# One core, two layers: routing and gates of an expert layer, with weights split two blocks ahead, TensorE in program order, 20 row dots in routing and gate copies in 16-byte runs

## Chip, cores and metric

One core of a Trainium2 chip runs the whole kernel. Its engines work side by side and wait for each other through semaphores: TensorE (PE, matrix products; PEld is its weight load), VectorE (DVE), ScalarE (ACT), GpSimd (POOL) and SyncE (SP, which here only issues DMAs). ACT and POOL issue DMAs too, from the same queue of instructions in which their other work stands. The metric is the device time of one execution in microseconds; less is better.

## The reference, cut

512 tokens of width 1024 pass two layers. Each layer is a mixer (a recurrence in the first, attention in the second) and then a feed-forward part with 16384 experts, of which each token uses 128. Only this part is touched:

```python
q = (xc @ q_w).reshape(TOKEN_CHUNK, PEER_HEADS, 2, PEER_HALF)
s1 = jnp.einsum('thd,hnd->thn', q[:, :, 0], subkey1)
s2 = jnp.einsum('thd,hnd->thn', q[:, :, 1], subkey2)
v1, i1 = lax.top_k(s1, PEER_TOPK)
v2, i2 = lax.top_k(s2, PEER_TOPK)
cand = (v1[..., :, None] + v2[..., None, :]).reshape(TOKEN_CHUNK, PEER_HEADS, PEER_TOPK * PEER_TOPK)
top_s, top_c = lax.top_k(cand, PEER_TOPK)
e1 = jnp.take_along_axis(i1, top_c // PEER_TOPK, axis=-1)
e2 = jnp.take_along_axis(i2, top_c % PEER_TOPK, axis=-1)
expert = e1 * PEER_KEYS + e2
g = jax.nn.softmax(top_s, axis=-1)
u = jnp.take(expert_u, expert, axis=0)
act = jax.nn.gelu(jnp.einsum('thkd,td->thk', u, xc), approximate=False)
return jnp.einsum('thk,thkd->td', g * act, jnp.take(expert_v, expert, axis=0))
```

## The kernel before

**Two ways to compute the experts.** Tokens are taken in four tiles of 128. The last tile is computed by gathering: for each of its 128 experts per token a row of `expert_u` is fetched by an indirect DMA and multiplied with the token on DVE, and the same for `expert_v`. The other three tiles (`nd` = 3, 384 tokens) are computed densely: all 16384 experts, 128 at a time, as matrix products, and what a token did not choose is multiplied with a gate of zero. Of these 384 tokens, 32 (`XT`) are a mixed case: their first product is done by gathering, in `looked_up`, as 32 dots (L1037) of 1024 numbers on 128 partitions. So the dense first product has 352 columns.

**float32 by halves.** Every float32 operand of PE is split into a rounded high part and a low rest; a product is three matmuls. Splitting a block of weights takes one ACT instruction (`whi`, L185) and one DVE subtraction (`wlo`, L187). `Stream` does this in the order of use: `take` hands out a block and first splits on to `ahead` blocks beyond it; there are four buffers of each half. The raw weights come in pairs of blocks, 1 MB, through SP.

**The part that is changed**, L1208 to L1221, runs once in each layer, between the search for the best keys (`queries`) and the loop over all experts (L1284). It goes over the 54 blocks of `FIRST[NEARLY:]`. For each it calls `first_up` (L831): `proj_t` makes the 24 matmuls of 128x352 (L513 to L515), ACT applies the gelu into `at` (L835, two buffers), and an ACT-issued DMA stores it to `ascr` (L836) for the loop that follows. After each block, `bg.pump(GP)` lets generators run whose work is mostly DVE's: each `yield` gives a cost, and the pump goes on until the costs used reach the credit, 5.35 per block. What is left at the end runs in `bg.finish()`. The generators, in order:

- `route(t)` for the four tiles (the tile with the 32 mixed tokens first): it turns positions among the candidates into the indices `e1`, `e2` by comparing with the constants `thr`, `row`, `col` and adding up (`route_half`), and makes the softmax `gt`.
- `looked_up`, dealt out between the steps of the others by `between_steps`: `natural` (L255, 16 transposing matmuls into one PSUM bank, L257 copies out) makes the tokens row-wise, then 32 dots. Their rows are fetched by POOL, 13 of them into buffers that the gates will use later, two per dot; the rest into three buffers `xr` once routing is over. At the end the results are copied together (L1042), scaled, and the largest is spread by one matmul (L1054) and copied to `most_all`, which the loop reads.
- `dense_gates(t)` for three tiles, eight passes each over 16 tokens, 24 passes in all. DVE compares with a ramp to get two sets of zeros and ones, `p2` (L1123) and `p1` (L1126), and multiplies `p1` with the two halves of the gate into `pg` (L1134, twice). `products` then multiplies `p2` and `pg` on PE, 32 matmuls of 128x128 (L1108) into four PSUM banks; ACT evicts each bank into `st` (L1110), 512 numbers per partition, written 64 bytes apart; `st` goes to `gscr` in DRAM by one ACT-issued DMA of 1 MB (L1112), and one eighth of it is kept by L1111. A pass's products are put after the next pass's `p2` and `p1` in the program.

The order in which one engine's instructions stand is decided by a scheduler when the kernel is built, by its own estimate of times; what is wrapped in `keep_in_program_order` (or `pin`) keeps its place in the program. PE's instructions in this part are not pinned before. The loop over experts (L1284) has its own background, the gathered tile, dealt out by `PUMPS`: a credit for a block whose first product must still be computed, and one for a block that was stored.

Of the kernel before, what the change touches and what calls it, by code (L numbers as in the profile page):

```python
# [17 lines left out]
S = 512  # L18
# [20 lines left out]
NEARLY = sum(EARLY)  # L39
PUMPS = ((4.55, 1.5), (4.2, 1.35))  # L40
AHEAD = 6
GP = 5.35
GSCALE = 32768.0
# [205 lines left out]

def natural(g, psum, h, tokens, out, half):  # L250

    ps = psum.tile([128, 4, 128], F32, name="nat", tag="tp", bufs=1)
    for k in range(4):
        for i, part in enumerate(h):
            g.nc.tensor.matmul(ps[:, k, :], tokens(part[:, half * 4 + k]), g.identr,  # L255
                               start=(i == 0), stop=(i == 1))
    g.nc.scalar.activation(out[:, half * 512:(half + 1) * 512].rearrange("p (a b) -> p a b", b=128), ps, AF.Copy)  # L257
# [247 lines left out]

def proj_t(g, psum, h, n=S, bank=None):

    nc = g.nc
    whi, wlo = g.stream.take()
    hhi, hlo = h  # L510
    ps = (psum.tile([128, S], F32, name="pacc", tag="acc") if bank is None else bank)[:, :n]
    for k in range(KD):
        nc.tensor.matmul(ps, whi[:, k, :], hhi[:, k, :n], start=(k == 0), stop=False)  # L513
        nc.tensor.matmul(ps, whi[:, k, :], hlo[:, k, :n], start=False, stop=False)  # L514
        nc.tensor.matmul(ps, wlo[:, k, :], hhi[:, k, :n], start=False, stop=(k == KD - 1))  # L515
    return ps
# [289 lines left out]
def peer(g, norm_fn, u, v, grow_fn, gate_rows, between, last_rows, nd, cost):  # L806
# [10 lines left out]
    with pool(tc, name="pk", bufs=1) as pk:  # L817
# [13 lines left out]
        def first_up(psum, c, ps=None):  # L831

            ps = proj_t(g, psum, h, NX) if ps is None else ps
            at = pa.tile([128, NX], F32, name="at", tag="at")
            A.activation(at, ps, AF.Gelu)  # L835
            nc.scalar.dma_start(ascr[FIRST.index(c)], at)  # L836
# [28 lines left out]
        HK = PH * QK  # L865
        thr = rs.tile([128, TOPK, HK], BF, name="thr")
        row = rs.tile([128, TOPK, HK], BF, name="rowlen")
        col = rs.tile([128, TOPK, HK], BF, name="col")

# [68 lines left out]
        def route_half(t, q):  # L938
# [15 lines left out]
            n = QK * (q + 1)  # L954
            shp = [128, n, HK]
            tab = [x[:, :n] for x in env["tab"]]
# [4 lines left out]
            ge, ge2 = (rs.tile([128, TOPK, HK], BF, name=x, tag=x)[:, :n] for x in ("ge", "ge2"))  # L961
            V.tensor_tensor(ge, posb.unsqueeze(1).to_broadcast(shp), thr[:, :n], op=OP.is_ge)
            V.tensor_tensor(ge2, ge, row[:, :n], op=OP.mult)
            V.tensor_tensor(ge, ge, tab[0], op=OP.mult)
            fold(ge, n, ranks(e[0], q))
            yield (6.0, 7.2)[q]
            j = rs.tile([128, HK], BF, name="j", tag="j")
            fold(ge2, n, j.rearrange("p (h k) -> p h k", h=PH))
            V.tensor_sub(j, posb, j)
            V.tensor_tensor(ge, j.unsqueeze(1).to_broadcast(shp), col[:, :n], op=OP.is_equal)  # L970
            V.tensor_tensor(ge, ge, tab[1], op=OP.mult)
            fold(ge, n, ranks(e[1], q))
            yield (5.5, 8.4)[q]

        def route(t):
# [16 lines left out]
            yield 2.2  # L992

        def looked_up(t, pu, pw, psum):
# [15 lines left out]
            def fetch(j):  # L1010
                if j < 13:
                    k = (0, 0, 1, 1, 2, 2, 3, 4, 4, 4, 4, 4, 4)[j]
                    if k == 4:
                        if j % 2:
                            env["pair"] = pw.tile([128, 2, D], F32, name="two", tag="st", bufs=3)
                        r = env["pair"][:, (j + 1) % 2]
                    else:
                        r = (pu if k == 3 else pw).tile([128, D], F32, name="rowx", tag=("p2", "pg0", "pg1", "p1")[k])
                else:
# [12 lines left out]
            for j in range(XT):  # L1032
                for _ in range(2):
                    if len(rows) < (XT if "xr" in env else 13):
                        fetch(len(rows))
                r = rows[j]
                pin(V.scalar_tensor_tensor(r, r, 1.0, hn, op0=OP.mult, op1=OP.mult, accum_out=act[:, j:j + 1]))  # L1037
                yield 1.35 if "xr" in env else 2.9
            A.activation(act, act, AF.Gelu)
# [11 lines left out]
            V.tensor_scalar(gt[own], back[own], inv[own], None, op0=OP.mult)  # L1051
            V.tensor_copy(back, most.to_broadcast([128, 128]))
            ps = psum.tile([128, 4, 128], F32, name="tp", tag="tp", bufs=1)
            T.matmul(ps[:, 0, :XT], back, g.ident[:, 128 - XT:], start=True, stop=True)  # L1054
            A.activation(most_all, ps[:, 0, :XT], AF.Copy)

        def between_steps(main, side, credit):
# [15 lines left out]
        def dense_gates(t, pu, pw, psum, todo):  # L1073
# [19 lines left out]
            pin(V.scalar_tensor_tensor(gp[1], tp[:, 2, :], GSCALE, gp[0], op0=OP.mult, op1=OP.subtract))  # L1093
            gdup = []
            for i in range(2):
                d = pu.tile(shp, F16, name=f"gdup{i}", tag=f"gdup{i}")
                A.activation(d, gp[i].unsqueeze(2).to_broadcast(shp), AF.Copy)
                gdup.append(d)
            yield 1.5

            def products(n, p2, pg):
                st = pw.tile([128, 128, 16], F32, name="st", tag="st", bufs=3)
                for q in range(4):
                    gps = psum.tile([128, 4, 128], F32, name="gps", tag="sps", bufs=4)
                    for r in range(4):
                        tk_ = q * 4 + r
                        for i in range(2):
                            T.matmul(gps[:, r, :], p2[:, tk_, :, :].rearrange("p a b -> p (a b)"), pg[i][:, :, tk_, :],  # L1108
                                     start=(i == 0), stop=(i == 1))
                    A.activation(st[:, :, q * 4:q * 4 + 4].rearrange("p e t -> p t e"), gps, AF.Copy, scale=1.0 / GSCALE)  # L1110
                A.activation(gts[0][:, n], st[:, 0:8, :], AF.Copy)  # L1111
# [5 lines left out]
            for b in range(8):  # L1117
# [10 lines left out]
                if todo:  # L1128
                    products(*todo.pop())
                    yield 0.1  # L1130
                pg = []
                for i in range(2):
                    x = pw.tile(shp, F16, name=f"pg{i}", tag=f"pg{i}")
                    pin(V.tensor_tensor(x, p1, spread(gdup[i]), op=OP.mult))  # L1134
                    pg.append(x)
                    yield 1.15
                todo.append((t * 8 + b, p2, pg))
# [64 lines left out]
        with pool(tc, name="ups", bufs=1, space=PSUM) as psum:  # L1202
# [540 lines left out]
```

## Time and profile before

| | us |
|---|---|
| median of 3 runs (3107.61 to 3116.07) | 3108.65 |
| the profiled execution | 3111.14 |
| its span | 3109.4 |
| around the span | 1.7 |
| granted clock, mean | 0.984 |

The span is divided, by what runs, into the recurrence, layer 0's queries, its routing and gates (437 to 744 us), its loop over experts (to 1516), attention, and the same three parts of layer 1 (routing and gates 2031 to 2338, the loop to the end). In the rows below a group is a line, an engine and an operation, with output and input names, shapes, count, busy us in total, mean ns of one, and then the idle time of that engine just before them and what ended it. ACTq marks a DMA issue in ACT's queue, with the time that the issue took. Instructions of one engine overlap a little, so a duration is somewhat longer than the distance to the next start.

### The profile page before, as it was taken

How to read it: one execution, taken by the hardware profiler on the slowest of the kernel's cores; microseconds unless marked ns; L12 is line 12 of the kernel's file. 1: busy time of each engine (PE TensorE's matmuls, PEld its weight loads, DVE VectorE, ACT ScalarE, POOL GpSimd, SP SyncE). 2: the span in 40 equal slices, each digit the busy share in tenths (PEclk: the TensorE clock that was granted, in tenths of full speed). 3: DMA queues.
4: the chain of work that ended last, by engine and by line, in shares of the span. 5: the costliest groups of instructions: out<-in, count | busy, mean ns of one | idle time of the engine just before them, and what ended most of it. 6: DMA issues, size and time to landing. Idle time of an engine off the chain costs nothing.

```text
span 3109.4 us, 45245 instructions
## 1 busy us (share of the span) xinstructions
PE 2987.0 (96%) x16232; PEld 2631.3 (85%) x16232; DVE 2618.9 (84%) x5368; ACT 1486.9 (48%) x2432; POOL 1053.1 (34%) x906
## 2 busy tenths in 40 slices
PE   8999999989999999999999999999889999999999
PEld 6778899878888888888777778999779888888887
DVE  8867987887988989999679878889886889888897
ACT  6664254677333333333458843255674333333332
POOL 1001422211655525664011003421204555445552
PEclk9999999989999999999999999999999999999999
DMA  7454347878999999998332133367979999999996
GB/s 294 176 186 168 111 150 295 271 250 286 418 383 383 393 358 387 386 383 338 136 113 83 63 149 128 116 254 254 286 241 363 363 385 378 374 347 383 361 361 247
DMA packets 307938, 855.28 MB, mean 275 GB/s; under 512 B 27296, under 2 KB 162496, under 8 KB 268928
## 3 DMA queue, kind: packets, MB, share of 16 engines
q1 hardware_dynamic: 67280, 388.77, 33.0%
q0 software_dynamic: 98624, 354.99, 30.2%
q10 hardware_dynamic: 141808, 108.63, 10.6%
q8 instruction: 127, 2.08, 0.3%
q14 instruction: 99, 0.81, 0.1%
HBM read 767.93 MB, written 83.51 MB: 274 GB/s over the span
## 4 chain that ended last, share of the span: by engine, by line
PE 50%; DVE 23%; DMA 9%; issue 8%; ACT 8%; ACTq 2%; POOL 0%; DVEq 0%; SPq 0%; POOLq 0%
PE vacc L1271 16%; PE pacc L515 9%; PE pacc L513 9%; PE pacc L514 8%; DMA at<-ascr 7%; DVE wlo L187 4%; DVE accg L1179 4%; DVE rows L1162 3%; ACT st L1110 2%; DVE mw L220 1%; ACTq L836 1%; ACT whi L185 1%; PE gps L1108 1%; DVE at L1257 1%; DVE wl L1264 1%
## 5 line engine op out<-in xcount | busy, mean ns | idle before, releaser
L515 PE MATMUL pacc<-hhi,wlo 128*128 128x352 f32 (+1 forms) x2600 | 892.6, 344 | 20.5 <-DVE wlo L187 20.3
L513 PE MATMUL pacc<-hhi,whi 128*128 128x352 f32 (+1 forms) x2600 | 898.0, 345 | 9.0 <-ACT at L835 5.8
L185 ACT ACTIVATE whi<-wraw 128x1024 fp32r<-128x1024 f32 (+1 forms) x646 | 661.7, 1033 | 494.1 <-PE pacc L514 272.9
L514 PE MATMUL pacc<-hlo,whi 128*128 128x352 f32 (+1 forms) x2600 | 892.4, 343 | 0.0
L187 DVE TENSOR_TENSOR wlo<-wraw,whi 128x1024 fp32r<-128x1024 f32 (+2 forms) x580 | 698.2, 1210 | 162.0 <-ACT whi L185 153.8
L1271 PE MATMUL vacc<-whi,wh 128*128 128x512 f32 x1536 | 598.3, 390 | 0.0
L1271 PE MATMUL vacc<-whi,wl 128*128 128x512 f32 x1536 | 597.7, 389 | 0.0
L1271 PE MATMUL vacc<-wlo,wh 128*128 128x512 f32 x1536 | 597.7, 389 | 0.0
L515 PEld LDWEIGHTS pacc<-hhi,wlo 128*128 128x128 f32 x2600 | 495.7, 191 | 50.6 <-DVE wlo L187 27.6
L513 PEld LDWEIGHTS pacc<-hhi,whi 128*128 128x128 f32 x2600 | 496.4, 191 | 40.2 <-ACT at L835 6.3
L514 PEld LDWEIGHTS pacc<-hlo,whi 128*128 128x128 f32 x2600 | 497.2, 191 | 26.0
L1261 ACT ACTIVATE wh<-at 128x384 fp32r<-128x384 f32 x256 | 134.2, 526 | 786.2 <-DVE at L1257 639.2
L1149 POOL DMA_INDIRECT rows<-in_l_v_dram,ei x256 | 370.9, 1449 | 306.5 <-DVE accg L1179 259.7
L1149 POOL DMA_INDIRECT rows<-in_l_u_dram,ei x256 | 371.4, 1451 | 269.5 <-DVE rows L1162 217.0
L1271 PEld LDWEIGHTS vacc<-whi,wl 128*128 128x128 f32 x1536 | 288.3, 188 | 60.2
L1271 PEld LDWEIGHTS vacc<-wlo,wh 128*128 128x128 f32 x1536 | 288.7, 188 | 55.8
L1271 PEld LDWEIGHTS vacc<-whi,wh 128*128 128x128 f32 x1536 | 288.4, 188 | 55.9
L1179 DVE SCALAR_TENSOR_TENSOR accg<-rows,act,accg 128x1024 f32<-128x1024 f32 x254 | 324.4, 1277 | 0.1
L1162 DVE SCALAR_TENSOR_TENSOR rows<-rows,hn 128x1024 f32<-128x1024 f32 x256 | 304.8, 1217 | 2.7 <-DMA rows<-in_l_u_dram,ei 2.6
L1257 DVE TENSOR_TENSOR at<-at,gtile 128x384 f32<-128x384 f32 x256 | 140.8, 552 | 151.8 <-DMA at<-ascr 144.9
L1110 ACT ACTIVATE st<-gps 128x512 f32<-128x512 f32 x192 | 185.0, 1105 | 70.8 <-PE gps L1108 50.7
L1021 POOL DMA_INDIRECT rowx<-in_l_u_dram,eix x52 | 75.5, 1452 | 354.7 <-DVE rowx L1037 187.5
(335 smaller groups left out, 3691.6 us busy)
## 6 DMA issues: line engine op xcount, KB each, us to landing
wraw<-in_l_uT_dram SPq DMA_DIRECT2D x128, 1024.0 KB
wraw<-in_l_vp_dram SPq DMA_DIRECT2D x128, 1024.0 KB
gscr<-st ACTq DMA_DIRECT2D x48, 1024.0 KB
gtile<-gscr SPq DMA_DIRECT2D x90, 512.0 KB
mw<-in_l_ffn_mw_dram POOLq DMA_DIRECT2D x48, 512.0 KB
ascr<-at ACTq DMA_DIRECT2D x136, 176.0 KB
at<-ascr ACTq DMA_DIRECT2D x136, 176.0 KB
mw<-in_l_mix_mw_dram POOLq DMA_DIRECT2D x32, 512.0 KB
```

What stands on the lines that cost most here:

```text
L185: self.pin(nc.scalar.activation(hi, raw, AF.Copy))
L187: self.pin((nc.gpsimd if self.on_pool else nc.vector).tensor_sub(lo, raw, hi))
L513: nc.tensor.matmul(ps, whi[:, k, :], hhi[:, k, :n], start=(k == 0), stop=False)
L514: nc.tensor.matmul(ps, whi[:, k, :], hlo[:, k, :n], start=False, stop=False)
L515: nc.tensor.matmul(ps, wlo[:, k, :], hhi[:, k, :n], start=False, stop=(k == KD - 1))
L1110: A.activation(st[:, :, q * 4:q * 4 + 4].rearrange("p e t -> p t e"), gps, AF.Copy, scale=1.0 / GSCALE)
L1149: i = nc.gpsimd.indirect_dma_start(out=rows, out_offset=None, in_=src, in_offset=bass.IndirectOffsetOnAxis(ap=ei[:, j:j + 1], axis=0))
L1162: V.scalar_tensor_tensor(r, r, 1.0, hn, op0=OP.mult, op1=OP.mult, accum_out=act[:, j:j + 1]))
L1179: i = V.scalar_tensor_tensor(acc, r, w, acc, op0=OP.mult, op1=OP.add)
L1257: pin(V.tensor_tensor(at.rearrange("p (b t) -> p b t", t=16), at.rearrange("p (b t) -> p b t", t=16), gts[c // 8][:, :, c % 8, :], op=OP.m ...
L1261: pin(A.activation(wh, at, AF.Copy))
L1271: T.matmul(acc[t][d], x[:, ts], y[:, d, :], start=(i == 0 and x is wh and y is vh), stop=(i == PK - 1 and x is wl))
```

## The change

- `proj_t` gets a `pin`; in this part the first matmul of each block keeps its place in the program, and so does the first gate matmul of each of the four banks in `products`.
- `g.stream.ahead` is 2 during this part, 3 again after it. `at` has four buffers.
- The credit `GP` is 4.81 by its formula; routing's costs and its dots are scaled by `RS` = 1.6. 20 of the 32 dots (`RX`) are to run in routing, from the same 13 buffers in rotation; a row is fetched after each dot, three ahead.
- `natural` in `looked_up` uses the four banks of the products. The matmul and copy for `most_all` become a generator of their own, `most_of`, behind all others.
- The two `pg` products are one of twice the size; the two `gdup` tiles are one.
- The evictions write four neighbouring numbers (16 bytes) at a time, and read PSUM in the order that this asks for.
- The constants `thr`, `row`, `col` are kept once and not once per head; DVE reads them with a repeated dimension.
- `PUMPS` of layer 0's loop: 4.55 and 1.5 become 4.35 and 1.42.

```diff
-PUMPS = ((4.55, 1.5), (4.2, 1.35))
+PUMPS = ((4.35, 1.42), (4.2, 1.35))
-GP = 5.35
+RX = 20
+RS = 1.6
+GP = ((54.4 + 1.3 * RX) * RS + 119.7 + 1.35 * (XT - RX)) / (NFIRST - 13)
...
-            at = pa.tile([128, NX], F32, name="at", tag="at")
+            at = pa.tile([128, NX], F32, name="at", tag="at", bufs=4)
...
-        thr = rs.tile([128, TOPK, HK], BF, name="thr")
+        thr = rs.tile([128, TOPK, QK], BF, name="thr")
...
-            V.tensor_tensor(ge, posb.unsqueeze(1).to_broadcast(shp), thr[:, :n], op=OP.is_ge)
-            V.tensor_tensor(ge2, ge, row[:, :n], op=OP.mult)
+            V.tensor_tensor(heads(ge), ranked(posb), fixed(thr), op=OP.is_ge)
+            V.tensor_tensor(heads(ge2), heads(ge), fixed(row), op=OP.mult)
...
-            yield (6.0, 7.2)[q]
+            yield RS * (2.75, 3.4)[q]
...
-                natural(g, psum, h, lambda x: x[:, ND - 128:ND], hn, half)
+                natural(g, psum, h, lambda x: x[:, ND - 128:ND], hn, half, "sps", 4)
...
-                for _ in range(2):
-                    if len(rows) < (XT if "xr" in env else 13):
-                        fetch(len(rows))
+                while len(rows) <= j:
+                    if "xr" in env:
+                        for n in range(RX, RX + 3):
+                            fetch(n)
+                    yield 0.1
                 r = rows[j]
                 pin(V.scalar_tensor_tensor(r, r, 1.0, hn, op0=OP.mult, op1=OP.mult, accum_out=act[:, j:j + 1]))
-                yield 1.35 if "xr" in env else 2.9
+                n = len(rows)
+                if n < (min(RX, j + 14) if n < RX or "xr" not in env else min(XT, max(RX, j + 1) + 3)):
+                    fetch(n)
+                yield 1.35 if "xr" in env else RS * 1.3
...
-                            T.matmul(gps[:, r, :], p2[:, tk_, :, :].rearrange("p a b -> p (a b)"), pg[i][:, :, tk_, :],
-                                     start=(i == 0), stop=(i == 1))
-                    A.activation(st[:, :, q * 4:q * 4 + 4].rearrange("p e t -> p t e"), gps, AF.Copy, scale=1.0 / GSCALE)
+                            m = T.matmul(gps[:, r, :], p2[:, tk_, :, :].rearrange("p a b -> p (a b)"),
+                                         pg[:, i].rearrange("p a (t b) -> p a t b", b=8)[:, :, tk_, :],
+                                         start=(i == 0), stop=(i == 1))
+                            if r == 0 and i == 0:
+                                tc.keep_in_program_order(m)
+                    A.activation(st[:, :, q * 4:q * 4 + 4], gps.rearrange("p t e -> p e t"), AF.Copy, scale=1.0 / GSCALE)
...
-                pg = []
-                for i in range(2):
-                    x = pw.tile(shp, F16, name=f"pg{i}", tag=f"pg{i}")
-                    pin(V.tensor_tensor(x, p1, spread(gdup[i]), op=OP.mult))
-                    pg.append(x)
-                    yield 1.15
+                pg = pw.tile([128, 2, 16, 128], F16, name="pg", tag="pg")
+                pin(V.tensor_tensor(pg, p1.rearrange("p a t b -> p a (t b)").unsqueeze(1).to_broadcast([128, 2, 16, 128]),
+                                    gdup[:, :, bs, :].rearrange("p i t b -> p i (t b)").unsqueeze(2).to_broadcast(
+                                        [128, 2, 16, 128]), op=OP.mult))
+                yield 2.3
...
-                bg = Background(parts[0], between_steps(itertools.chain(*parts[1:-1]), looked_up(nd - 1, pu, pw, psum), (6.8, 3.3)),
-                                parts[-1])
+                bg = Background(parts[0], between_steps(itertools.chain(*parts[1:-1]), looked_up(nd - 1, pu, pw, psum), (RS * 1.85, 4.6)),
+                                parts[-1], most_of(psum))
+                g.stream.ahead = 2
                 for c in FIRST[NEARLY:]:
-                    first_up(banks, c)
+                    first_up(banks, c, proj_t(g, banks, h, NX, pin=tc.keep_in_program_order))
...
                 bg.finish()
+                g.stream.ahead = 3
```

More of the change, by code (lines that the diff above doesn't have):

```diff
@@ L247, in row_of, with natural @@
     return row
-def natural(g, psum, h, tokens, out, half):
-    ps = psum.tile([128, 4, 128], F32, name="nat", tag="tp", bufs=1)
+def natural(g, psum, h, tokens, out, half, tag="tp", bufs=1):
+    ps = psum.tile([128, 4, 128], F32, name="nat", tag=tag, bufs=bufs)
     for k in range(4):
@@ L503, in proj_early, with proj_t @@
     return ps
-def proj_t(g, psum, h, n=S, bank=None):
+def proj_t(g, psum, h, n=S, bank=None, pin=lambda x: x):
     nc = g.nc
@@ L512, in proj_t @@
     for k in range(KD):
-        nc.tensor.matmul(ps, whi[:, k, :], hhi[:, k, :n], start=(k == 0), stop=False)
+        (pin if k == 0 else lambda x: x)(
+            nc.tensor.matmul(ps, whi[:, k, :], hhi[:, k, :n], start=(k == 0), stop=False))
         nc.tensor.matmul(ps, whi[:, k, :], hlo[:, k, :n], start=False, stop=False)
@@ L865, in peer @@
         HK = PH * QK
-        thr = rs.tile([128, TOPK, HK], BF, name="thr")
-        row = rs.tile([128, TOPK, HK], BF, name="rowlen")
-        col = rs.tile([128, TOPK, HK], BF, name="col")
+        thr = rs.tile([128, TOPK, QK], BF, name="thr")
+        row = rs.tile([128, TOPK, QK], BF, name="rowlen")
+        col = rs.tile([128, TOPK, QK], BF, name="col")
         def constants(rows):
@@ L954, in route_half, with heads, ranked, fixed @@
             n = QK * (q + 1)
-            shp = [128, n, HK]
+            shp = [128, n, PH, QK]
+            def heads(x):
+                return x.rearrange("p r (h k) -> p r h k", h=PH)
+            def ranked(x):
+                return x.rearrange("p (h k) -> p h k", h=PH).unsqueeze(1).to_broadcast(shp)
+            def fixed(x):
+                return x[:, :n].unsqueeze(2).to_broadcast(shp)
             tab = [x[:, :n] for x in env["tab"]]
@@ L969, in route_half @@
             V.tensor_sub(j, posb, j)
-            V.tensor_tensor(ge, j.unsqueeze(1).to_broadcast(shp), col[:, :n], op=OP.is_equal)
+            V.tensor_tensor(heads(ge), ranked(j), fixed(col), op=OP.is_equal)
             V.tensor_tensor(ge, ge, tab[1], op=OP.mult)
             fold(ge, n, ranks(e[1], q))
-            yield (5.5, 8.4)[q]
+            yield RS * (2.5, 3.85)[q]
         def route(t):
@@ L991, in route @@
                 e.append(ei)
-            yield 2.2
+            yield RS * 1.1
         def looked_up(t, pu, pw, psum):
@@ L1010, in fetch @@
             def fetch(j):
[L1011 to L1016, printed above, removed]
-                    else:
-                        r = (pu if k == 3 else pw).tile([128, D], F32, name="rowx", tag=("p2", "pg0", "pg1", "p1")[k])
+                if j < RX:
+                    tag, n = (("p2", 0), ("p2", 0), ("p1", 0), *(("pg", i % 2) for i in range(4)),
+                              *(("st", i % 2) for i in range(6)))[j % 13]
+                    if tag in ("p2", "p1"):
+                        r = (pu if tag == "p1" else pw).tile([128, D], F32, name="rowx", tag=tag)
+                    else:
+                        if n == 0:
+                            env["pair"] = pw.tile([128, 2, D], F32, name="two", tag=tag, bufs=3 if tag == "st" else 2)
+                        r = env["pair"][:, n]
                 else:
@@ L1052, in looked_up, with most_of @@
             V.tensor_copy(back, most.to_broadcast([128, 128]))
+            env["back"] = back
+        def most_of(psum):
             ps = psum.tile([128, 4, 128], F32, name="tp", tag="tp", bufs=1)
-            T.matmul(ps[:, 0, :XT], back, g.ident[:, 128 - XT:], start=True, stop=True)
+            T.matmul(ps[:, 0, :XT], env["back"], g.ident[:, 128 - XT:], start=True, stop=True)
             A.activation(most_all, ps[:, 0, :XT], AF.Copy)
+            yield 0.1
         def between_steps(main, side, credit):
```

6 lines of the change are left out of this document (2 added, 4 removed).

## Prediction

> **What bounds the kernel now.** I read the totals first, then stretches of time, then, inside the stretch that is not dense, the groups of each engine, the order of time on ScalarE (ACT), and the waits. The page opens with this, and its chain of waits names what ended last:
>
> ```profile
> span 3109.4 us, 45245 instructions
> PE 2987.0 (96%) x16232; PEld 2631.3 (85%) x16232; DVE 2618.9 (84%) x5368; ACT 1486.9 (48%) x2432; POOL 1053.1 (34%) x906
> PE 50%; DVE 23%; DMA 9%; issue 8%; ACT 8%; ACTq 2%; POOL 0%; DVEq 0%; SPq 0%; POOLq 0%
> ```
>
> TensorE (PE) at 96% looks like the end of the matter, but it is an average. The windows view, by stage, for layer 0 (routing; gates; the loop over experts) and then layer 1:
>
> ```profile
> 437.00:548.00 111.00, 108.60 (x663) 108.30 (x662) 92.75 (x224) 60.26 (x78) 19.12 (x16) 0.97 0.69 251
> 548.00:744.00 196.00, 171.34 (x1447) 162.06 (x1446) 166.22 (x174) 139.68 (x188) 26.13 (x16) 0.91 0.83 265
> 744.00:1516.00 772.00, 759.28 (x3763) 665.64 (x3762) 673.66 (x914) 290.61 (x519) 393.84 (x288) 1.00 0.93 365
> 2031.00:2142.00 111.00, 108.60 (x663) 108.22 (x662) 92.81 (x223) 60.43 (x79) 18.49 (x16) 0.97 0.71 251
> 2142.00:2338.00 196.00, 167.54 (x1441) 157.35 (x1440) 165.89 (x173) 139.17 (x187) 25.62 (x16) 0.93 0.83 264
> 2338.00:3109.00 771.00, 758.82 (x3742) 664.97 (x3741) 655.50 (x866) 284.77 (x505) 372.15 (x273) 1.00 0.93 357
> ```
>
> Columns are length, then busy us and count of PE, PEld, DVE, ACT, POOL, then granted clock, DMA share, GB/s. Routing (111 us) is full on PE. The gates stage (196 us) is full on nothing that is counted: PE lacks 25 us and its clock fell to 0.91, VectorE (DVE) is at 85%, ACT at 71%. The loop (772 us) has PE at 98%. So there is room only in the gates, twice. What fills them is on ACT, whose DMA issues are not counted as busy. Its groups from 548 to 744 us, and its order of time:
>
> ```profile
> L1110 ACT ACTIVATE st<-gps 128x512 f32<-128x512 f32 x96 | 92.6, 1107 | 34.7 <-PE gps L1108 26.7 <-issue 7.6 <-ACT st L1110 0.2
> L257 ACT ACTIVATE hn<-nat 128x512 f32<-128x512 f32 x2 | 1.2, 616 | 0.0
> 561.96 3.02 ACTq L836 DMA_DIRECT2D ascr<-at  x1
> 578.48 3.83 ACT L1110 ACTIVATE st<-gps 128x512 f32<-128x512 f32 x4 [1.69 <-PE gps L1108]
> 582.35 0.39 ACTq L1112 DMA_DIRECT2D gscr<-st  x1
> 582.78 8.00 ACTq L836 DMA_DIRECT2D ascr<-at  x1
> 590.82 1.06 ACT L185 ACTIVATE whi<-wraw 128x1024 fp32r<-128x1024 f32 x1 [8.03 <-issue]
> 736.43 1.46 ACTq L836 DMA_DIRECT2D ascr<-at  x1
> L836 ACTq DMA_DIRECT2D ascr<-at x136: 321/327/7995, 278.4 to 2330.5; - x136
> 671.36 2.91 ACTq L1042 DMA_DIRECT2D back<-actx  x4
> L835 ACT ACTIVATE at<-pacc 128x352 f32<-128x352 f32 x28 | 13.1, 468 | 2.7 <-issue 2.4 <-PE pacc L515 0.3
> ```
>
> [...] In layer 0's gates 17 ascr issues are longer than 0.45 us (the first at 561.96, the last at 736.43); together they are 36 us over the median of 0.33 (min/median/max of L836). ACT's account of the 196 us is: busy 139.7, 23 gscr issues x 0.38 = 8.7, 28 ascr issues x 0.33 = 9.2, stalls 36, the four issues of L1042 2.9. That is 196.5; an issue can overlap the end of an ACTIVATE a little. **ACT, in its own order, is what the gates stage waits for**; half of its busy time are the 96 evictions.
>
> **The change, part by part.** I call the 54 weight blocks of this part "blocks" and the 24 passes over 16 tokens "gate blocks".
>
> *Evictions (L1110).* Same 512 numbers from PSUM, written in runs of four instead of single numbers 64 bytes apart. An ACT copy of the same size out of PSUM to unbroken rows takes 616 ns (L257, above). I take 0.60: 96 x (1.107 - 0.60) = 48.7 us less ACT work per layer. Bounds: nothing, if the read, now in steps of 512 bytes, costs what the write did; and +48.7, if it costs that on top. No row reads PSUM so. The nearest row that reads in steps, from SBUF and each number eight times, is L950:
>
> ```profile
> L950 ACT ACTIVATE tab<-d 128x1024 bf16<-128x1024 f32 x4 | 4.2, 1053 | 5.2 <-DVE d L946 5.2
> L185 ACT ACTIVATE whi<-wraw 128x1024 fp32r<-128x1024 f32 x27 | 28.5, 1057 | 30.5 <-PE pacc L514 22.1 <-issue 4.5 <-PE pacc L515 3.4
> ```
>
> It costs what the unbroken copy of 1024 costs (1053 against 1057), so steps on the read side were free there; that is why I take the low price. The Trainium skill speaks against it: "Advanced Engine Details and Errata", section PSUM Cachelines, wants every two consecutive elements of PSUM contiguous for best throughput, and here none are. By that rule the saving is lost, which is the first rival below; no row here shows it either way.
>
> *Split two ahead, four `at` buffers, natural on four banks.* In routing ACT waits 22.1 us for PE to free the fourth weight buffer (L185 row above). Two more, from the waits of 437 to 548 us:
>
> ```profile
> ACT at L835 <- DMA ascr<-at: 9.3, 5, 3.2
> PE nat L255 <- ACT hn L257: 2.4, 1, 2.4
> 490.00:510.00 20.00, 20.00 (x126) 20.00 (x125) 17.07 (x41) 9.12 (x13) 0.00 (x0) 1.00 0.83 305
> ```
>
> The two ACT waits go, but stand beside a full PE (126 matmuls in 20 us), so they are worth nothing in routing. The 2.4 us of PE go and count. What less lead costs: two blocks are 2 x 24 x 20/126 = 7.6 us of PE, and a gate block's products lie between; the longest ACT stall is 8.00. Just covered; if not, some 3 us of new waits per layer.
>
> *Credits and dots.* DVE pieces are handed out by cost. Before, routing held 4 x 29.3 + 12 x 2.9 = 152 units at 5.35 per block: 28.4 blocks. After, 1.6 x (54.4 + 1.3 x 20) = 128.6 at 4.81: 26.7. So 1.7 blocks and 8 dots change sides. Routing by PE: 26.7 x 24 x 20/126 = 101.7, plus 16 matmuls of natural, 1.8 at their spacing of 0.11: 103.5. DVE beside it (steps of 1.14, the spacing of the rows below): 92.75 + 8 x 1.14 - 1.7 x 1.14 = 99.9. Two near ends, and DVE at 97%, which no stage of this kernel reaches; I take **106 for 111**.
>
> ```profile
> 622.67 1.22 DVE L1123 TENSOR_TENSOR p<-iota_f,edup 128x2048 f16<-128x2048 f16 x1
> 623.81 1.22 DVE L1126 TENSOR_TENSOR p<-iota_f,edup 128x2048 f16<-128x2048 f16 x1
> 714.60 0.27 PE L255 MATMUL nat<-identr,hlo 128*128 128x128 f32 x1
> 714.72 0.27 PE L255 MATMUL nat<-identr,hhi 128*128 128x128 f32 x1
> L963 DVE TENSOR_TENSOR ge<-ge,rowlen 128x1024 bf16<-128x1024 bf16 x4 | 2.8, 693 | 0.2
> L963 DVE TENSOR_TENSOR ge<-ge,rowlen 128x512 bf16<-128x512 bf16 x4 | 1.7, 423 | 0.1
> ```
>
> *Compact constants.* L962, L963 and L970 keep their sizes and runs of eight; I take no change. If they ran at half rate they would double, 3 x (2.8 + 1.7) = 13.5 us more DVE and routing 113. The shorter memsets lie on POOL, idle there.
>
> *One fetch per dot.* POOL's fetches no longer stand behind the dots; only fetches queue there. A row is asked for three dots ahead, some 12 us at one dot per block in routing; the first row before was issued at 466.5 and used at 472.9. So no wait; if bursts of dots outrun it, DVE waits a few us, with routing's wlo and PE behind it.
>
> ```profile
> 466.48 1.07 POOL L1021 DMA_INDIRECT rowx<-in_l_u_dram,eix  x1 [37.19 <-DVE j L936]
> 472.93 1.22 DVE L1037 SCALAR_TENSOR_TENSOR rowx<-rowx,hn 128x1024 f32<-128x1024 f32 x1
> PE gps L1108 <- DVE pg L1134: 17.1, 10, 4.1
> 561.24 1.96 PE L1108 MATMUL gps<-pg,p 128*128 128x128 f16 x32
> q0 software_dynamic: 2304, 8.39, 13.6%
> 570.00:590.00 20.00, 20.00 (x184) 19.36 (x183) 17.41 (x19) 10.47 (x14) 5.04 (x3) 1.00 1.01 316
> ```
>
> *TensorE in program order, one pg product.* A pinned gate matmul that waits holds the next block's matmuls behind it, and ACT's `at` behind those. But in program order the products of a pass follow the p2 and p1 of the next, 2.3 us of DVE after their pg; now some directly follow it and wait (17.1 us). I count this wait as gone, and one 4096 product for two of 2048 as no gain (0 to 0.1 us each). `most_of` goes behind everything; its one matmul and copy cost under 0.5 us at the end.
>
> *Gates, summed.* ACT: 196 - 48.7 + 1.7 x (1.07 + 0.47 + 0.33) = 150. DVE: 166.2 - 8 x 1.14 + 1.7 x 1.14 = 159. PE at full clock: 27.3 blocks x 3.81 + 24 x 1.8 (561.24) + 1 = 148. DMA, at the 316 GB/s of a stretch that is full (570 to 590): 196 us x 265 GB/s = 51.9 MB, less 4 rows of 0.52 MB, plus 1.7 blocks of 0.7: 51.0 MB, 161 us. Four floors within 13 us of each other; the old one lay at 196 alone. The kernel's fullest stretches run DVE at 0.93:
>
> ```profile
> 1300.00:1350.00 50.00, 50.00 (x249) 43.90 (x248) 46.69 (x51) 18.40 (x33) 31.86 (x21) 1.00 0.98 380
> 1450.00:1520.00 70.00, 68.93 (x330) 58.57 (x329) 52.27 (x77) 29.86 (x54) 3.98 (x8) 1.00 0.48 181
> ```
>
> I take 159 / 0.91 = **175 for 196**. Ends: 161, and 188 if the ring stalls, which I leave at 36, grow by half and DVE falls to 0.85, as now.
>
> *Pace of layer 0's loop.* 56 blocks x 4.55 + 64 x 1.5 = 351 credits for 336 units before; 334 after. The row work ended early (DMA 0.48 in the last stretch) and will now reach the end. But layer 1 already runs 322 for 319, and its loop lacks the same 12 us of PE (771 - 758.8, and 772 - 759.3). I take **-2**, between -8 and +3.
>
> **Sum.** Per layer (111 - 106) + (196 - 175) = 26; twice 52, with the loop 54. The profiled execution took 3111.1 (span 3109.4 and 1.7 around it), 2.5 above the median of 3108.65: 3111.1 - 54 = 3057, or **3054.6** on the median. Its own ends: routing 104 to 110, gates 161 to 188, loop -8 to +3 give 3108.65 - 92 = 3017 to 3108.65 - 15 = 3094.
>
> **Rivals.**
> 1. *The stepped read costs what the stepped write did.* Evictions stay at 1.1, ACT's account stays 196 + 3 = 199, and nothing that DVE or PE gains shows. Against it speaks L950; for it, that L950 is not PSUM. (106 + 199) against 307 and the loop: 3108.65 - 4 - 2 = 3103.
> 2. *It doesn't do what it says: the DMA ring takes the time.* The same 24 MB of gscr in a shorter stage; if the ascr issues come as close behind the gscr issues as at 582.78, and stall 3.0 us on average instead of 36 / 28 = 1.3, ACT has 48 us back. Same time as before, 3109. For it: DMA share 0.83 now and over 0.9 then; against: fewer rows fall in the gates, and the worst stalls lie where they were.
> 3. *Slower: the read costs on top of the write.* 1.6 us an eviction: ACT 199 + 49 = 248 in each gates stage, so 3108.65 + 2 x (52 - 5) - 2 = 3201. It decides as soon as an eviction takes over 1.13 us: rival 1 leaves 2 us a layer, and 96 x 0.02 eats them.
> 4. *Better:* all four floors are met, 3017 or below.
>
> **How the numbers follow.** About 0.3% (9 us) is what a measurement of this kernel tells from no change. Forecast 0.63, rival 1 0.14, rival 2 0.10, rival 3 0.08, rival 4 0.05. Faster by over 0.3% is the forecast, rival 4 and some of rival 1, which straddles the bound: 0.74. Within: the rest of rival 1 and most of rival 2, 0.15. Slower: rival 3 and a part of 2, 0.11. For 8 in 10 the range takes the forecast's own and reaches over rival 1: 3017 to 3104.
>
> **What would show it.** Right: L1110 near 600 ns; ACT's busy time in the gates below 100; granted clock over 0.95 there; no wait of PE for pg; DVE over 0.9. Wrong: L1110 at 1.1 or more (rivals 1, 3); ACTq L836 over 80 us a layer (rival 2); DVE waiting for rowx; PE waiting for wlo in routing.

## The result and the profile after

The changed kernel takes **3034.12 us** (median of 4 runs, 3030.05 to 3043.34) against 3112.36 us for the kernel before in the same comparison (4 runs, 3107.61 to 3119.78): a ratio of 0.9751, 95% interval 0.9719 to 0.9782. The gain is 78 us where 54 were forecast; the time lies within the range. The profiled execution took 3034.66 us.

The page's totals and chain of waits, of the kernel after:

```profile
span 3032.9 us, 45201 instructions
PE 2952.4 (97%) x16232; PEld 2608.2 (86%) x16232; DVE 2612.9 (86%) x5320; ACT 1409.5 (46%) x2432; POOL 1063.3 (35%) x906
PE 49%; DVE 25%; DMA 13%; issue 8%; ACT 5%; POOL 1%; ACTq 0%; DVEq 0%; SPq 0%; POOLq 0%
```

ACT lost 77 us of busy time, and its issues (ACTq) left the chain; DVE and the transfers took over its share. Where the time went shows best at the gate products on DVE, whose first and last start mark the gates stage of layer 0. Routing, ahead of it, is marked by the last sum of candidates (`cand`) of the search for the best keys. Two rows of before, then the same two of after (duration min/median/max in ns, then the first and the last start):

```profile
L883 DVE TENSOR_TENSOR cand<-vals,vals x8: 178/184/187, 310.8 to 433.6; 128x32 f32<-128x32 f32 x8
L1134 DVE TENSOR_TENSOR pg<-p,gdup x48: 1214/1218/1227, 552.0 to 738.6; 128x2048 f16<-128x2048 f16 x48
```

```profile
L886 DVE TENSOR_TENSOR cand<-vals,vals x8: 178/186/193, 313.9 to 436.8; 128x32 f32<-128x32 f32 x8
L1156 DVE TENSOR_TENSOR pg<-p,gdup x24: 2279/2286/2294, 550.9 to 701.6; 128x4096 f16<-128x4096 f16 x24
```

The gates stage begins 1.1 us earlier and lasts 150.7 us for 186.6. Followed through the program:

| | before | after | later minus earlier in all | in this part |
|---|---|---|---|---|
| last `cand` sum of layer 0 | 433.6 | 436.8 | +3.2 | +3.2 |
| first pg product of layer 0 (routing ends) | 552.0 | 550.9 | -1.1 | -4.3 |
| last pg product of layer 0 (gates end) | 738.6 | 701.6 | -37.0 | -35.9 |
| last `cand` sum of layer 1 | 2027.2 | 1996.1 | -31.1 | +5.9 |
| first pg product of layer 1 | 2145.5 | 2108.8 | -36.7 | -5.6 |
| last pg product of layer 1 | 2332.2 | 2259.5 | -72.7 | -36.0 |
| end of the span | 3109.4 | 3032.9 | -76.5 | -3.8 |

Nearly all of it is the two gates stages. The two routings gave 4.3 and 5.6 us, and the last loop 3.8. Ahead of routing in layer 0, and from the gates of layer 0 to the routing of layer 1, 3.2 and 5.9 us went the other way; of the kernels below, the one with nothing but the pins, which leaves these parts as they were, lies 4.0 and 4.1 us above the kernel before there too, so this is not shown to be an effect of the change. The windows view of after, routing, gates and loop of layer 0, then gates and loop of layer 1, with the columns as before; last, routing of layer 0 once more, cut at the same distance from the marks as the first window of before:

```profile
440.00:550.00 110.00, 106.54 (x653) 105.70 (x652) 102.08 (x245) 58.93 (x78) 29.86 (x23) 0.97 0.74 284
550.00:708.00 158.00, 154.72 (x1460) 151.43 (x1460) 152.87 (x131) 101.54 (x188) 19.71 (x9) 1.00 0.95 303
708.00:1486.00 778.00, 762.50 (x3762) 667.79 (x3760) 674.37 (x914) 290.60 (x520) 396.02 (x288) 1.00 0.94 363
2108.00:2266.00 158.00, 154.76 (x1461) 151.49 (x1460) 152.65 (x131) 101.77 (x188) 19.20 (x9) 1.00 0.96 304
2266.00:3032.00 766.00, 756.09 (x3737) 661.97 (x3735) 656.72 (x867) 284.67 (x505) 374.63 (x273) 1.00 0.93 360
440.20:546.90 106.70, 103.24 (x631) 102.40 (x631) 98.97 (x240) 56.35 (x74) 29.86 (x23) 0.97 0.76 292
```

The stage that was full on nothing is now full on PE (154.72 of 158 us, 98%), on DVE (152.87, 97%) and nearly on the transfers (0.95), at full clock. ACT, which I held for the limit, is busy for 101.5. Its groups in that stretch:

```profile
L1134 ACT ACTIVATE st<-gps 128x512 f32<-128x512 f32 x96 | 50.4, 603 | 13.4 <-PE gps L1129 7.1 <-DMA back<-actx 2.8 <-issue 2.3
L838 ACT ACTIVATE at<-pacc 128x352 f32<-128x352 f32 x29 | 13.5, 465 | 40.1 <-PE pacc L518 40.1
L259 ACT ACTIVATE hn<-nat 128x512 f32<-128x512 f32 x2 | 1.2, 592 | 0.0
```

An eviction takes 603 ns, about as much as the unbroken copy (592). ACT now stands 40.1 us for PE before the gelu: it has slack. The long ascr issues (over 0.45 us) have nearly gone: where 17 of them had 36 us of excess in layer 0's gates, 9 now have 7 us. In the whole program the longest fell from 7995 ns to 3026:

```profile
L839 ACTq DMA_DIRECT2D ascr<-at x136: 321/326/3026, 281.5 to 2263.3; - x136
```

### The profile page after: what moved, and what is told of

It reads as the page before. It is cut to its first block, busy times and chain, and to the rows that moved or that the text cites. A ratio compares the mean times of both kernels' runs of the same rounds, so it can differ in the third digit from the quotient of the medians.

```text
span 3032.9 us, 45201 instructions
## 1 busy us (share of the span) xinstructions
PE 2952.4 (97%) x16232; PEld 2608.2 (86%) x16232; DVE 2612.9 (86%) x5320; ACT 1409.5 (46%) x2432; POOL 1063.3 (35%) x906
## 4 chain that ended last, share of the span: by engine, by line
PE 49%; DVE 25%; DMA 13%; issue 8%; ACT 5%; POOL 1%; ACTq 0%; DVEq 0%; SPq 0%; POOLq 0%
PE vacc L1296 13%; DMA at<-ascr 9%; PE pacc L518 9%; PE pacc L516 9%; PE pacc L517 9%; DVE accg L1202 5%; DVE wlo L189 4%; DVE rows L1185 3%; PE gps L1129 2%; DVE wl L1289 1%; DVE pg L1156 1%; DVE at L1282 1%; ACT whi L187 1%; DVE mw L222 1%; DMA wraw<-in_l_vp_dram 1%
## 5 line engine op out<-in xcount | busy, mean ns | idle before, releaser
L518 PEld LDWEIGHTS pacc<-hhi,wlo 128*128 128x128 f32 x2600 | 492.3, 189 | 48.7 <-DVE wlo L189 25.5
L189 POOL TENSOR_TENSOR wlo<-wraw,whi 128x1024 fp32r<-128x1024 f32 (+1 forms) x62 | 125.3, 2032 | 185.4 <-ACT whi L187 185.4
L1034 POOL DMA_INDIRECT rowx<-in_l_u_dram,eix x36 | 58.3, 1618 | 246.6 <-DVE rowx L1052 145.7
```

Of the source, the lines that this page charges most:

```text
L189: self.pin((nc.gpsimd if self.on_pool else nc.vector).tensor_sub(lo, raw, hi))
```

## Experiments

Twelve kernels ran, each compared with the kernel before on the same chip. "Gates" below is the time from the first to the last start of a pg product, in layer 0 where no layer is named: 186.6 us before, 150.7 after. "Routing" is the time from the last `cand` sum to the first pg product: 118.4 before, 114.1 after. Each kernel has its own line numbers; the names of the tiles tell what a row is.

### 1 and 2: the evictions alone, and all but the evictions

```diff
-  A.activation(st[:, :, q * 4:q * 4 + 4].rearrange("p e t -> p t e"), gps, AF.Copy, scale=1.0 / GSCALE)
+  A.activation(st[:, :, q * 4:q * 4 + 4], gps.rearrange("p t e -> p e t"), AF.Copy, scale=1.0 / GSCALE)
```

The first run has this in the kernel before; the second has it undone in the changed kernel.

> The kernel before with the 16-byte evictions alone. Theory A (ACT's own account bounds the gates stage): 48 us of ACT work leave each gates stage, which falls from 196 to about 178 us, where VectorE's 166 us and the waits for pg hold it; 3109 - 36 = 3073, between 3063 and 3083. Theory B (the order of TensorE's work is what counted, the evictions were covered): less than 10 us gained, 3100 or more.

> The changed kernel with the old evictions, single numbers 64 bytes apart. Theory A: ACT's busy time in the gates goes from 102 back to 150 us, with 18 us of issues and 8 to 36 of stalls 176 to 204 us against a stage of 158: 18 to 46 us a layer are lost, 3034 + 36 to 92, so 3070 to 3126. Theory B: order keeps most of the gain, 3050 or less.

Measured: evictions alone 3068.37 us, ratio 0.9871 (0.9840 to 0.9903); all but the evictions 3052.13 us, 0.9801 (0.9778 to 0.9825). So alone they bring 1.3%, 40 us, and on top of the rest 0.5%, 16 us. The windows of the gates stage, first of the kernel with the evictions alone, then of the one with all but them:

```profile
552.00:718.00 166.00, 153.74 (x1387) 144.68 (x1386) 160.50 (x168) 94.63 (x177) 26.92 (x16) 0.98 0.93 298
```

```profile
550.00:711.00 161.00, 150.48 (x1397) 146.34 (x1396) 148.88 (x129) 131.20 (x175) 19.73 (x9) 0.99 0.91 289
```

and ACT's eviction group in the second:

```profile
L1134 ACT ACTIVATE st<-gps 128x512 f32<-128x512 f32 x90 | 87.8, 1116 | 21.8 <-issue 11.2 <-PE gps L1129 5.5 <-DMA back<-actx 4.0
```

The first row confirms the size and the place: without any other part of the change the stage falls to 166 us and DVE reaches 97% of it. The second row refutes half of my account: with evictions of 1116 ns the stage falls to 161 us all the same, and the time of 3052.13 lies below the range of theory A and just above that of theory B. Between the same marks ACT is busy for 131 us in the kernel before and in this one, and yet the second stage is 25 us shorter. The waits show how ACT holds the stage: DVE waits for its copies. First of the kernel before, then of the one with the old evictions:

```profile
DVE wlo L187 <- ACT whi L185: 12.9, 10, 4.0
DVE gp L1092 <- ACT edup L1089: 9.0, 2, 7.9
```

```profile
DVE wlo L189 <- ACT whi L187: 7.9, 7, 3.6
DVE gp L1115 <- ACT edup L1112: 3.5, 2, 2.9
```

These waits fall from 22 us to 11 by the rest of the change and to 2.5 in the whole change, whose stage is another 10 us shorter. So two cures, the evictions and something in the rest, each work alone and overlap. What in the rest it is was not isolated: the pins, the split and the dots are taken out of the change below, for 6 and 7 us and, at the best rate, 12, but the single pg product, the four `at` buffers, the compact constants and the place of `most_of` never ran alone.

### 3: the ascr stores out of ACT's queue

```diff
-            nc.scalar.dma_start(ascr[FIRST.index(c)], at)
+            nc.gpsimd.dma_start(ascr[FIRST.index(c)], at)
```

> The kernel before with the ascr stores issued by POOL, so that they never stand behind gscr in ACT's queue; evictions as before. Theory A: the 36 us of stalls and 9 us of issues leave ACT in each gates stage: 150 us of ACT work, the stage near 178 us, 3073 in all (3063 to 3088). Rival: the stalls lie in time in which ACT would have waited for pg or PE anyway, so no change, 3100 or more.

Measured on the kernel before: 3085.85 us, 0.9900 (0.9876 to 0.9925), at the edge of what was expected. The ascr issues in ACT's queue, stalls and plain issues together, were worth some 31 us when nothing else is changed. From POOL's queue none stalls; the row of the issues in this run, then the stage, with ACT still at 134.79 us of busy time:

```profile
L836 POOL DMA_DIRECT2D ascr<-at x136: 542/554/619, 280.9 to 2309.9; - x136
556.00:730.00 174.00, 156.85 (x1396) 148.44 (x1395) 162.33 (x171) 134.79 (x180) 42.74 (x43) 0.96 0.88 287
```

### 4: the old pace of the loops

```diff
-PUMPS = ((4.35, 1.42), (4.2, 1.35))
+PUMPS = ((4.55, 1.5), (4.2, 1.35))
```

> The changed kernel with layer 0's old pace of background work (4.55, 1.5). Theory P: the slower pace lets the row work run to the end of the loop, and the load of x behind it becomes late; the old pace gives back 4 to 9 us, 3025 to 3030. Rival: the 7 us that layer 0's loop got longer are due to something else, 3034 within 3.

Measured: 3036.13 us, 0.9740 (0.9718 to 0.9762), against 0.9751 for the full change. The theory of a gain by the old pace falls; the pace of layer 0's loop is worth nothing that these runs can tell.

### 5 to 8: TensorE in program order, and the split two ahead

The pins are taken out of the changed kernel (5), and put alone into the kernel before (8); the split is set back to three ahead in the changed kernel (6); and both are taken out of it (7).

```diff
-                    first_up(banks, c, proj_t(g, banks, h, NX, pin=tc.keep_in_program_order))
+                    first_up(banks, c)
...
-                            if r == 0 and i == 0:
-                                tc.keep_in_program_order(m)
...
-                g.stream.ahead = 2
```

> The changed kernel without the two pins on TensorE, all else as changed. Theory A2: the waits of TensorE for pg and the closer distance of ascr to gscr on ACT come back in part, 5 to 15 us a layer, 3034 + 10 to 30: 3044 to 3064. Rival (pins are worth nothing once ACT has time): 3034 within 4.

> The kernel before with the two pins on TensorE alone. Theory A2 (formed after the first four runs: of the 196 us of the gates stage ACT's own work fills about 170, and some 25 are waits made by TensorE's order, products set right behind their pg): the waits for pg go, each gates stage falls to about 172 us, 3110 - 48 = 3062, between 3050 and 3080. Rival (the two-ahead split or the moved dots gave what the old evictions kept of the gain, the pins nothing): 3100 or more.

> The changed kernel with the split three ahead as before. Theory A2: ACT waits for TensorE at the split and stands before the evictions, but it has some 40 us of slack in each gates stage now; 3034 to 3042. Rival (the two-ahead split is a main term): 3050 or more.

> The changed kernel with neither TensorE in program order nor the weights split two blocks ahead (three ahead, as before). Each alone was worth 7 to 8 us (3041.91 and 3041.19 against 3034.12). If the two are separate: 3046 to 3052 us. Rival: they cure the same waits, and both together are worth no more than one: 3038 to 3044 us.

| | us | ratio (95%) | gates, layers 0 and 1 |
|---|---|---|---|
| the change | 3034.12 | 0.9751 (0.9719 to 0.9782) | 150.7, 150.7 |
| without pins | 3041.91 | 0.9770 (0.9744 to 0.9795) | 156.4, 153.1 |
| three ahead | 3041.19 | 0.9774 (0.9750 to 0.9797) | 160.1, 156.5 |
| without both | 3044.11 | 0.9798 (0.9756 to 0.9841) | 158.1, 156.6 |
| pins alone, on before | 3117.97 | 1.0008 (0.9992 to 1.0024) | 187.2, 182.6 |

Each is worth some 6 to 7 us by the ratios, with intervals that overlap that of the change, so by the times alone neither is shown; the traces agree in direction, since the stage is longer in each of the three. With the split three ahead routing is 4.0 and 1.8 us shorter, so a part of what its gates lose is only moved. Whether the two add up stays open: the last but one row lies between the two expectations and its runs spread from 3039 to 3061 us. On the kernel before the pins do nothing (its second gates stage is 4 us shorter, the routing ahead of it 9 us longer). They do not even take away the wait that I thought they would; from the waits of the gates stage, of the kernel with pins alone and of the changed kernel without pins (us in total, times, longest):

```profile
PE gps L1109 <- DVE pg L1137: 25.5, 11, 6.4
```

```profile
PE gps L1129 <- DVE pg L1154: 2.2, 1, 2.2
```

PE's wait for pg was 17.1 us before. It grows with the pins alone, and is nearly gone without them once the rest is in place.

### 9 to 11: the dots back among the gates

13 dots in routing, as before, and 19 among the gates, which are dealt out there at one for so much due work of the gates: 4.6 in the change (9), 3.3 as in the kernel before (10), 2.3 (11).

```diff
-RX = 20
+RX = 13
...
-                bg = Background(parts[0], between_steps(itertools.chain(*parts[1:-1]), looked_up(nd - 1, pu, pw, psum), (RS * 1.85, 4.6)),
+                bg = Background(parts[0], between_steps(itertools.chain(*parts[1:-1]), looked_up(nd - 1, pu, pw, psum), (RS * 1.85, 3.3)),
```

> The changed kernel with RX = 13 in place of 20 (the credit follows by its formula). VectorE bounds the changed gates stage (156 of 161 us): 7 dots of 1.14 us come back to it, 8 us a layer, and routing, where TensorE is full, gives some 3 back: 3034 + 6 to 16, so 3040 to 3050. Rival (only the sum over both parts counts): 3034 within 4.

> The changed kernel with 13 row dots in routing again, the others dealt among the gates at one for 3.3 us of due work, as in the kernel before (the run with 13 and 4.6 took 3076.66 us, because the dots ended at 664.7 us instead of 628.9 and the transposes of the third tile then waited 17 us for its gates). Theory L (it is the lateness of the last dot that costs): by 14 dots of 1.3 us less due time each the last dot comes some 18 us earlier than at 4.6, near 646 us, which still holds up the third tile a little; 3036 to 3050 us. Rival D (more dots and row fetches among the gates cost VectorE and the transfers their time, wherever they end): 5 to 7 more dots of 1.3 us in each of two layers and the transfers' share above 0.95; 3055 us or more.

> As the run before, with the dots dealt at one for 2.3 us of due work, so that the last ends near 630 us, where it ends in the changed kernel. Theory L: no wait of a transpose for the third tile's gates is left, and 3030 to 3045 us. Rival D: the row fetches now crowd into the first half of the gates, VectorE waits for rows, and the time is 3055 us or more, no better than with 3.3.

| 13 dots in routing, one per | us | ratio (95%) | last dot in layer 0 | gates, layer 0 |
|---|---|---|---|---|
| 4.6 | 3076.66 | 0.9888 (0.9854 to 0.9922) | 663.5 | 180.6 |
| 3.3 | 3054.08 | 0.9812 (0.9780 to 0.9844) | 645.7 | 168.5 |
| 2.3 | 3048.97 | 0.9788 (0.9753 to 0.9823) | 618.4 | 164.2 |
| (the change: 20, 4.6) | 3034.12 | 0.9751 (0.9719 to 0.9782) | 627.7 | 150.7 |

The first result was far from what was expected, and its waits told why: among the longest of the gates stage, of the kernel with 13 dots and 4.6,

```profile
PE tp L1108 <- DVE gt L1069: 17.0, 1, 17.0
ACT actx L1057 <- DVE rowx L1052: 8.6, 1, 8.6
DVE rowx L1052 <- DMA rowx<-in_l_u_dram,eix: 4.1, 1, 4.1
```

and from its windows:

```profile
650.00:700.00 50.00, 32.99 (x296) 32.32 (x294) 37.54 (x39) 24.53 (x43) 2.75 (x1) 0.80 0.67 206
```

The third tile's gates `gt` can be scaled only when all 32 dots are done, and its transposes (L1108) stand in PE's order ahead of other work. Dots that end late stop PE for 17 us, and DVE behind it; in the 50 us around it PE ran for 33, at a clock of 0.80. The two other runs confirm that lateness is a cause, and that it is not the only one. Their windows of the gates, at 4.6, 3.3 and 2.3:

```profile
543.00:724.00 181.00, 157.84 (x1441) 154.22 (x1440) 158.75 (x143) 98.42 (x179) 31.95 (x15) 0.94 0.89 281
```

```profile
542.00:711.00 169.00, 157.98 (x1444) 154.44 (x1443) 159.37 (x146) 97.71 (x180) 29.33 (x16) 0.98 0.95 305
```

```profile
542.00:707.00 165.00, 157.55 (x1446) 154.10 (x1445) 159.56 (x146) 98.17 (x180) 30.64 (x16) 0.99 0.96 312
```

The same work (PE 158, DVE 159) fits into 181, 169 or 165 us, by when the last dot comes: that is 31 us of the 43 that the first of these kernels loses against the change (by the ratios, 0.9888 less 0.9788, and 0.9888 less 0.9751, of 3110 us). The other 12 us, by ratios whose intervals overlap, are in the trace too: at 2.3 routing is 7 us shorter than in the change (106.9 for 114.1) and the gates are 13.5 longer (164.2 for 150.7), 6 us a layer. The dots' own time is one part of it. The other is that the credit per block follows from `RX`, so that with fewer dots in routing fewer blocks are done there: 30 blocks fall between the first and the last pg product, for 28 in the change. The two were not separated. The two later runs fell between the two expectations: lateness is the larger part, the load among the gates the smaller.

### 12: a version that might be better

DVE is busy for 93% of routing and 97% of the gates, and POOL has time. Every fourth block's low part is subtracted on POOL.

```diff
-                for c in FIRST[NEARLY:]:
+                for n, c in enumerate(FIRST[NEARLY:]):
+                    g.stream.on_pool = n % 4 == 1
...
+                g.stream.on_pool = False
```

> The changed kernel with every fourth weight block's low part subtracted on GpSimd instead of VectorE in routing and gates. VectorE was busy for 97% of routing and of the gates. Theory V (VectorE's work sets both stages): some 13 blocks of about 1.2 us leave it, about 6 us in each layer: 3018 to 3028 us. Rival: TensorE, busy for 98% of the gates, or a low part that GpSimd finishes late holds the stage where it is or longer: 3032 us or more.

Measured: 3058.60 us, 0.9822 (0.9790 to 0.9854), some 22 us worse than the change by the ratios, as the rival had it. Routing is 6 to 7 us longer and the gates are 9 us longer, in both layers. The groups on DVE from routing to the end of the gates, first of this kernel, then of the change:

```profile
L1156 DVE TENSOR_TENSOR pg<-p,gdup 128x4096 f16<-128x4096 f16 x24 | 59.1, 2463 | 0.4
L189 DVE TENSOR_TENSOR wlo<-wraw,whi 128x1024 fp32r<-128x1024 f32 x43 | 52.1, 1218 | 4.8 <-ACT whi L187 4.8
L1147 DVE TENSOR_TENSOR p<-iota_f,edup 128x2048 f16<-128x2048 f16 x24 | 33.9, 1414 | 0.8 <-PE gps L1129 0.8
L1052 DVE SCALAR_TENSOR_TENSOR rowx<-rowx,hn 128x1024 f32<-128x1024 f32 x18 | 26.2, 1458 | 5.0 <-DMA rowx<-in_l_u_dram,eix 5.0
```

```profile
L189 DVE TENSOR_TENSOR wlo<-wraw,whi 128x1024 fp32r<-128x1024 f32 x54 | 65.8, 1219 | 6.4 <-ACT whi L187 6.0 <-issue 0.4
L1156 DVE TENSOR_TENSOR pg<-p,gdup 128x4096 f16<-128x4096 f16 x24 | 54.9, 2287 | 0.4
L1147 DVE TENSOR_TENSOR p<-iota_f,edup 128x2048 f16<-128x2048 f16 x24 | 29.2, 1218 | 0.0
L1052 DVE SCALAR_TENSOR_TENSOR rowx<-rowx,hn 128x1024 f32<-128x1024 f32 x18 | 21.9, 1218 | 0.0
```

DVE drops 13.7 us of wlo, and three groups alone grow by 13.2 (4.2 + 4.7 + 4.3). The timeline shows where from, first POOL, then DVE:

```profile
554.17 3.36 POOL L189 TENSOR_TENSOR wlo<-wraw,whi 128x1024 fp32r<-128x1024 f32 x1 [10.01 <-ACT whi L187]
```

```profile
555.22 4.46 DVE L1156 TENSOR_TENSOR pg<-p,gdup 128x4096 f16<-128x4096 f16 x1
```

The pg product that starts at 555.22, while POOL subtracts until 557.53, takes 4.46 us instead of 2.28: it is longer by 2.2, about the 2.3 us that POOL still needed. Of the seven subtractions in the gates of layer 0, six stretch one DVE instruction each by 2.1 to 2.2 us. The Trainium skill, "SBUF — State Buffer", section SBUF: two separate sides, describes such a thing: a GpSimd instruction that reads SBUF and a DVE instruction with two SBUF inputs exclude each other for a whole instruction. This trace agrees. In routing there is more: two dots waited 5.0 us for their rows, which POOL fetches (the L1052 row of this kernel), and PE then waited 7.6 us for a low part that DVE had to subtract behind them. How the 22 us divide between the two was not tested.

No run was measurably faster than the change.

## Why the prediction was right or wrong, step by step

**"ACT, in its own order, is what the gates stage waits for."** Half right. Relieving ACT by the evictions alone brought 40 us, and by moving its ascr issues 31, so ACT did hold the stage. But the account of 196.5 us that seemed to prove it was too long: it added all issues, 56.8 us, to all busy time, with the remark that an issue "can overlap the end of an ACTIVATE a little". Of ACT's 56 us of idle time in that stage only 24 ended with an issue; 32 ended with PE, 26.7 of them in the L1110 row that stood beside the account. (The evictions are also not half of ACT's busy time but two thirds, 92.6 of 139.7.) In the run with the old evictions, ACT's busy time of 131.2, 23 gscr issues and 29 ascr issues at the prediction's prices (18.3) and about 26 of stalls make 176, in 161 us. An overlap stands in the timeline of the change:

```profile
638.74 0.63 ACT L1134 ACTIVATE st<-gps 128x512 f32<-128x512 f32 x1
638.91 2.74 ACTq L839 DMA_DIRECT2D ascr<-at  x1
641.69 0.60 ACT L1134 ACTIVATE st<-gps 128x512 f32<-128x512 f32 x1 [2.33 <-issue]
```

The issue starts inside the eviction, and 2.33 of its 2.74 us hold ACT up. So a part of the 196 us was time in which ACT waited for others, which leaves room for causes off ACT.

**Evictions 1.107 to 0.60 us.** Right: 0.603. Rivals 1 and 3 are out. The row that I went by (L950, a read in steps from SBUF that costs nothing) carried over to PSUM. The rule of the Trainium skill that I set against it ("Advanced Engine Details and Errata", section PSUM Cachelines) did not hold for this copy on ACT.

**Ring stalls "which I leave at 36".** Wrong in size: 7. They did not grow in a shorter, denser stage (rival 2 is out; the transfers' share did rise to 0.95). They go with how closely an ascr issue follows a gscr issue. In the gates of layer 0 before, 19 ascr issues began within 3.1 us after the start of a gscr issue, and 17 of them were long; of the 9 others none was. In the change 5 began so close, and 2 of them were long; 7 others were, most of them by less than 1 us. That the 1 MB transfer itself is what holds the issue is not shown. The sum of the stalls is 31 us with the evictions alone, 25 in the change without pins, 35 in the change with three ahead. Why the whole change brings them to 7 was not isolated; with the old pace in the loop, which does not touch this part, it was 15.

**Gates, "159 / 0.91 = 175".** This step failed most. Measured in the same way it is 196 - 35.9 = 160: the stage came down to its floors, the lower end that I gave and my fourth rival's case in this stage. The floors themselves were near: DVE 152.9 busy for 159, PE 154.7 for 148 (29 blocks fell there, not the 27.3 that the credits gave; by the same credits the kernel before would have had 25.6, and its L835 row shows 28). The factor was wrong. I took DVE's share from the fullest stretches of the kernel before, none of which was limited by DVE; here, with next to no waits left (2.5 us for ACT), it ran at 97%, and with the evictions alone, too. And the transfers' floor of 161 was no wall: 9 rows were fetched in the stage (POOL's count in the windows), not 12, and 158 us x 303 GB/s make 47.9 MB instead of 51.0.

**Routing 106 for 111.** Right. From mark to mark it lost 4.3 us in layer 0 and 5.6 in layer 1; in a window cut like that of before it is 106.7 us for 111. PE was busy there for 103.2 of the 103.5 that I added up, with 631 matmuls for 663 (1.3 blocks fewer, where the credits gave 1.7), and DVE for 99.0 of 99.9. It does not show in the start of layer 0's gates, because routing itself began 3.2 us later in this profile.

**Waits.** The natural wait of 2.4 us went, as predicted. ACT's wait for the fourth weight buffer did not go; from the waits of routing, of the change:

```profile
ACT whi L187 <- PE pacc L517: 33.8, 16, 2.5
```

It grew from 22.1, and cost nothing, as predicted, since it stands beside a full PE. "Just covered" was right of the shorter lead, and perhaps cautious: two ahead came out 7 us faster than three, within the intervals. PE's wait for pg went from 17.1 us to 2.8, as counted, but not through the pins alone: by themselves they raised it to 25.5, and without them it was 2.2.

**Compact constants, one fetch per dot, one pg.** Right. L975 is the line that was L963, at 693 and 423 ns:

```profile
L975 DVE TENSOR_TENSOR ge<-ge,rowlen 128x1024 bf16<-128x1024 bf16 x4 | 2.8, 706 | 0.1
L975 DVE TENSOR_TENSOR ge<-ge,rowlen 128x512 bf16<-128x512 bf16 x4 | 1.7, 422 | 0.0
```

No dot waited for a row (the idle time before L1052 in the group above is 0.0), and the single pg product is 2286 ns for twice 1218.

**Pace of the loop, -2.** Not distinguishable from nothing (run 4). From the gates of layer 0 to the routing of layer 1 the profile lost 5.9 us, with the old pace 3.5, and the last loop, whose pace did not change, gained 3.8; with the pins alone, and the old loops, the first figure is 4.1 and the second 1.2, so little of either is the pace.

**The sum.** Forecast 26 us per layer, found 40.2 in layer 0 and 41.6 in layer 1: routing as forecast, and 15 us more from each gates stage, whose term was sized wrong by the factor for DVE. The 81.8 us of the two layers and the 3.8 of the last loop, less the 9.1 that went the other way in parts that the forecast did not price, make the 76.5 of the span. So the total is nearer to the forecast than the gates term is, by time lost elsewhere, and that is luck.

## What to carry to other kernels

Before an engine's queue is called the bound because its busy time and its issues add up to the stage, look whether issues run beside its instructions, count what ended its idle time, and take one other cause away: here two cures, each worth 40 to 60 us alone, brought 78 together. When a stage becomes limited by an engine, do not take its share from stretches in which something else held it up: DVE reached 97% here, not 91%. Compare a stage from its own first mark to its last, since what lies ahead of it can shift by some us. And ask of every piece of work that is dealt out among other work who needs its last result: the same dots, put at different rates, changed the time by some 30 us.

## What was not expected of the hardware

- ACT writing single float32 numbers 64 bytes apart takes 1107 to 1116 ns for 512 per partition, and 603 when four neighbours are written together, although it then reads PSUM in steps of 512 bytes; the unbroken copy takes 592 to 616.
- A GpSimd subtraction stretches a DVE instruction that it meets by about what it still has to run: 4.46 us instead of 2.28. With thirteen subtractions of 2.94 us in layer 0, and as many blocks in layer 1, the kernel is 22 us longer, although DVE has as many instructions of 1.22 us less.
- A store of 176 KB issued from ACT's queue, usually in 0.33 us, took up to 8.00 us when it followed a 1 MB store of the same queue within 3.1 us; issued from POOL's queue it took 0.54 to 0.62 us in all 136 cases.
